# Splitting the weights of the feed-forward products between the two sides of SBUF

## The chip, the cores and the metric

The kernel runs on one core of a Trainium2 chip. The metric is the device time of one execution in microseconds (us). Engines: PE does the matmuls, DVE the elementwise work on vectors, ACT casts and activation functions, POOL a share of the elementwise work, and SP issues all the loads and stores (its queue is called SPq in the trace). Each engine works through its own instructions in a fixed order that was laid down when the program was built, and waits on semaphores of the others.

## The reference

One layer of an encoder for a sequence of 2048 tokens with 1024 channels, in float32: a windowed attention (16 query heads, 4 key heads, 128 tokens to either side, with a bias and a sink), and a dense feed-forward layer. Each of the two is wrapped in two RMS norms, with shift, scale and gate from a conditioning vector. The feed-forward, which the change touches, is

```
h = rmsnorm(x) * (1 + scale) + shift          # 2048 x 1024
a, b = split(h @ w_in)                        # first products, w_in 1024 x 5632
y = (silu(a) * b) @ w_out                     # last products, w_out 2816 x 1024
out = x + gate * rmsnorm(y)
```

## The kernel before, in words

All data lie transposed, channels on the 128 partitions. Every f32 operand of a product is split into a high and a low part (`split`, lines 153 to 155: ACT casts the high part, DVE subtracts it from the source for the low part), and one product of 128x128 weights with 512 tokens is then three matmuls (`three`, lines 147 to 151: high by high, high by low, low by high).

The products of the feed-forward are done by Strassen's scheme with seven products instead of eight. The class `Block` (line 731) is one output tile of both halves of the columns: it loads raw weights (`raw`, lines 737 to 740), forms the sums s1, s2, s3, s4 of their quarters on DVE (lines 744 to 747), splits seven weight tiles (line 752), and then does seven steps (`step`, line 755): step i multiplies weight a11, s2, a12, s3, s1, a22, s4 with operand b11, t2, b21, t3, t1, t4, b22, in this order, into one PSUM tile `pc0` to `pc6` out of a pool of six (`psC`). `take` evicts it.

* First products: class `Hidden` (line 779), 22 blocks for each half of the tokens, with four pairs of weight and operand tiles a step, so 12 matmuls a step and 84 a block. Names end in `i<half>_<block>`: `pc4_i0_1` is step 4 of block 1 of half 0, `wiri` is its raw weight tile, `ws1_i0_1` the split weight s1. Operands of half 0 are `hb110_k`, `ht20_k`, ..., four tiles each, loaded and split by `Operands.load` (line 724). In the trace they read `hb` and `ht`, since buffer numbers are left out.
* Last products: class `Outs` (line 921), for every part of the inner dimension (2 or 3 pairs of tiles, `MD` = 3 at most) four blocks; names end in `o<half>_<part>_<block>`. Results of the parts are added up in tiles `z<half>_<block>_<step>` (line 942).
* A tail `pl` (line 1077 on): the last part's products without Strassen's scheme for the last two column chunks, with weights `wl` and operands `gls`.

Ahead of the first products, PE ends the last output projection of the attention: eight tiles `py3_0` to `py3_7` (operands `ol3_k`, weights `wo`). Its pools stand on the right of SBUF and are closed at `lasto.close()` (line 882), so a tile that is opened on the right after it waits until these tiles are no longer read. Interleaved with the first blocks there is a background chain of DVE, POOL, ACT and a few matmuls (`late`, tiles `nhil`, `nstl`, `lr`, `ly`), the norms of the later column chunks; a tile `u2` and others of `take` stand in between on DVE.

SBUF is used as two stacks, left and right. In the first products the weights have two pools, `wi0` (left, open early) and `wi1` (right), which blocks use in turn, seven split tiles in each. Operands b11 and t2 lie in `hA` (left), b21 in its own pool and t3 with t1 in another (both left), t4 and b22 in `hB` (right). In the last products one ring of eleven split weight tiles is on the left, with operands b11 and t2; the other five operands are on the right. Left pools of the first products are closed after step 4 (of steps 0 to 6) of the last `Hidden` block, right ones after step 6; the loads for the last products into that place wait for it.

The order of all instructions on each engine is set by a scheduler that ranks by program order and by the offsets of `tc.high_priority`.

Of the kernel before, what the change touches and what calls it, by code (L numbers as in the profile page):

```python
# [18 lines left out]
P = 128  # L19
# [54 lines left out]
def encoder_layer(ctx, tc, a):  # L74
# [626 lines left out]
    wi = [open_pool(early, "wi0"), None]  # L701
    hA = open_pool(early, "hA", KT // 2)
    wbufs = 7
# [6 lines left out]
    class Operands:  # L710
# [20 lines left out]
    class Block:  # L731
# [3 lines left out]
        def __init__(self, ops, i, u, wa, wb):  # L735
            self.ops, self.u, m = ops, u, ops.m
            pl = wi[i % len(wi)]
# [10 lines left out]
            src = dict(sm_, a11=a11, a12=a12, a22=a22)  # L748
# [127 lines left out]
    b21p = open_pool(early, "b21", K2)  # L876
    t3p = open_pool(early, "t3", K2)
# [23 lines left out]
    for i in range(5):  # L901
        hid.step(i)
# [109 lines left out]
    with tc.high_priority(offset=400):  # L1012
        ops.load(*OPERANDS[2:])
# [22 lines left out]
    gs, wl = {}, []  # L1036
    for j in range(CPH):
        c = NCH - CPH + j
        for k in range(m):
            gs[c, k] = t = (hA if k < 2 else hB).tile([P, 2, CH], F32R, tag=OPERANDS[k], name=f"gls{c}_{k}")  # L1040
            sp.dma_start(f(t[:, 1]), g_d[-1][(t0 + k) // 2][f"b{k % 2 + 1}{j + 1}"])
            split(t[:, 0], t[:, 1], f(t[:, 1]), dve)
    for n in range(KT):
        raw = wi[0].tile([P, 2, 2 * MD * P], F32, tag="raw", name=f"wlr{n}").rearrange("p a b -> p (a b)")[:, :m * P]
        sp.dma_start(raw, a["w_out"][n, :, t0:t0 + m].rearrange("p k c -> p (k c)"))
        t = hB.tile([P, 2, CH], F32R, tag=("t1", "t4", "b22")[n // 3], name=f"wl{n}")
# [86 lines left out]
```

## Time and profile before

| what | value |
|---|---|
| median of three runs (2163.89, 2169.1, 2169.4) | 2169.1 us |
| the profiled execution | 2166.07 us, of it 2164.3 us span |
| PE busy | 2055.8 us (95% of the span) |
| DVE busy | 1649.8 us (76%) |
| ACT busy | 1076.4 us (50%) |
| POOL busy | 737.5 us (34%) |

Times within the profile count from the start of the span. The attention with its projections takes until about 821 us, the first products until 1688 us, the last products until 2098 us, the tail's matmuls until 2145 us, and then the last sums and stores. A row of the timeline has the start, the duration, the engine, the line, the operation, what it writes and reads, and how many alike it groups; in square brackets how long the engine sat idle before it and for whom. A row of the table by windows has the busy time and the count of instructions of each engine in a stretch, the granted clock of PE as a share of full speed, and what the DMA did.

### The profile page before, as it was taken

How to read it: one execution, taken by the hardware profiler on the slowest of the kernel's cores; microseconds unless marked ns; L12 is line 12 of the kernel's file. 1: busy time of each engine (PE TensorE's matmuls, PEld its weight loads, DVE VectorE, ACT ScalarE, POOL GpSimd, SP SyncE). 2: the span in 40 equal slices, each digit the busy share in tenths (PEclk: the TensorE clock that was granted, in tenths of full speed). 3: DMA queues.
4: the chain of work that ended last, by engine and by line, in shares of the span. 5: the costliest groups of instructions: out<-in, count | busy, mean ns of one | idle time of the engine just before them, and what ended most of it. 6: DMA issues, size and time to landing. Idle time of an engine off the chain costs nothing. (4 is left out here: it accounts for less than half of the span.)

```text
span 2164.3 us, 28995 instructions
## 1 busy us (share of the span) xinstructions
PE 2055.8 (95%) x9366; PEld 1666.6 (77%) x9366; DVE 1649.8 (76%) x2933; ACT 1076.4 (50%) x2125; POOL 737.5 (34%) x687
## 2 busy tenths in 40 slices
PE   6898999989989989999999999999999999998996
PEld 4786877878867768878887877888888788877886
DVE  7656767665676669876878897767673888999987
ACT  4546666577777746343434342333332844465422
POOL 3404343367778723434344422222221000220030
PEclk8999999999999989999999999999999999999998
DMA  8877665576667695545455764332231644438442
GB/s 279 261 254 253 184 182 175 159 282 233 227 199 245 189 347 206 183 148 162 138 178 194 257 220 142 112 106 94 98 117 54 210 153 138 141 129 280 161 132 103
DMA packets 200516, 396.35 MB, mean 183 GB/s; under 512 B 20091, under 2 KB 62124, under 8 KB 195244
## 3 DMA queue, kind: packets, MB, share of 16 engines
q1 hardware_dynamic: 199788, 393.97, 54.7%
q8 instruction: 74, 1.21, 0.2%
q14 instruction: 78, 0.64, 0.1%
q10 hardware_dynamic: 576, 0.52, 0.1%
HBM read 270.65 MB, written 123.76 MB: 182 GB/s over the span
## 5 line engine op out<-in xcount | busy, mean ns | idle before, releaser
L437 DVE CUSTOM_DVE_ANT_0 pr<-s,bias,nsink 128x384 f32<-128x384 f32 (+1 forms) x256 | 149.3, 596 | 91.5 <-PE s L432 74.3
L149 PE MATMUL pc_i<-ht,ws_i 128*128 128x512 f32 x528 | 207.2, 393 | 2.1 <-DVE b_i L799 1.5
L150 PE MATMUL pc_i<-ht,ws_i 128*128 128x512 f32 x528 | 206.9, 392 | 0.0
L151 PE MATMUL pc_i<-ht,ws_i 128*128 128x512 f32 x528 | 206.9, 392 | 0.0
L439 ACT ACTIVATE pr<-pr,nm 128x385 f32<-128x385 f32 (+1 forms) x256 | 153.8, 603 | 71.3 <-DVE nm L437 64.3
L815 POOL TENSOR_TENSOR p_i<-p_i,u_i 128x512 f32<-128x512 f32 x44 | 71.5, 1625 | 310.7 <-DVE u_i L802 153.6
L445 POOL TENSOR_SCALAR pr<-pr,rs 128x384 f32<-128x384 f32 (+1 forms) x256 | 147.4, 601 | 83.0 <-DVE rs L443 82.9
L946 POOL TENSOR_TENSOR z<-z,z 128x512 f32<-128x512 f32 x32 | 52.5, 1654 | 359.2 <-DVE z L942 342.3
L432 PE MATMUL s<-k,q 128*128 128x384 f32 (+1 forms) x512 | 136.1, 359 | 20.2 <-DVE nm L437 13.6
L149 PE MATMUL pc_i<-hb,wa_i 128*128 128x512 f32 x352 | 139.1, 395 | 2.0 <-DVE u_i L789 2.0
L150 PE MATMUL pc_i<-hb,wa_i 128*128 128x512 f32 x352 | 138.7, 394 | 0.0
L151 PE MATMUL pc_i<-hb,wa_i 128*128 128x512 f32 x352 | 138.7, 394 | 0.0
L155 DVE TENSOR_TENSOR plo<-t,phi 128x512 fp32r<-128x512 f32 x184 | 121.7, 685 | 16.2 <-ACT phi L154 14.7
L154 ACT CAST wa_i<-wiri 128x512 fp32r<-128x512 f32 x132 | 81.8, 620 | 102.2 <-PE pc_i L151 94.7
L154 ACT CAST ws_i<-s_i 128x512 fp32r<-128x512 f32 x132 | 81.6, 618 | 102.5 <-PE pc_i L151 98.7
L432 PEld LDWEIGHTS s<-k,q 128*128 128x128 f32 x512 | 86.6, 193 | 44.9 <-DVE nm L437 27.8
L149 PEld LDWEIGHTS pc_i<-ht,ws_i 128*128 128x128 f32 x528 | 99.3, 188 | 25.5 <-DVE b_i L799 2.2
L151 PEld LDWEIGHTS pc_i<-ht,ws_i 128*128 128x128 f32 x528 | 99.2, 188 | 22.4
L150 PEld LDWEIGHTS pc_i<-ht,ws_i 128*128 128x128 f32 x528 | 99.2, 188 | 22.2
L455 PE MATMUL t<-ident,pr 128*128 128x128 f32 x736 | 113.1, 273 | 3.1 <-POOL pr L445 2.4
L149 PE MATMUL py<-ol,wo 128*128 128x512 f32 x256 | 103.3, 405 | 11.9 <-ACT wo L154 7.4
L155 DVE TENSOR_TENSOR ws_i<-s_i,ws_i 128x512 fp32r<-128x512 f32 x132 | 104.6, 792 | 10.9 <-ACT ws_i L154 10.7
(320 smaller groups left out, 6142.8 us busy)
## 6 DMA issues: line engine op xcount, KB each, us to landing
wiri<-w_in SPq DMA_DIRECT2D x88, 512.0 KB, 4.8
ada<-ada_w SPq DMA_DIRECT2D x40, 512.0 KB, 4.9
wiro<-w_out SPq DMA_DIRECT2D x48, 384.0 KB, 3.9
q_d<-e SPq DMA_DIRECT2D x64, 256.0 KB, 3.9
q<-q_d SPq DMA_DIRECT2D x16, 1024.0 KB, 5.8
wo<-wo_d SPq DMA_DIRECT2D x16, 1024.0 KB, 5.7
g_d_b<-p_i SPq DMA_DIRECT2D x44, 256.0 KB, 4.7
g_d_t<-p_i SPq DMA_DIRECT2D x40, 256.0 KB, 2.0
```

The costliest lines, as they stand in the source:

```text
L149: pe.matmul(ps, w[0], h[0], start=first, stop=False)
L150: pe.matmul(ps, w[0], h[1], start=False, stop=False)
L151: pe.matmul(ps, w[1], h[0], start=False, stop=last)
L154: act.copy(hi, src)
L155: return eng.tensor_tensor(lo, src, f(hi), ALU.subtract).ins
L432: m = pe.matmul(ps[:, :n], q[:, h, jb * P:(jb + 1) * P], kk[:, i, (jb + j0) * P:(jb + j1) * P], start=i == 0, stop=i == 1)
L437: red = dve.tensor_tensor_reduce(pr[:, h, :n], ps[:, :n], bias[g][:, h, j0 * P:j1 * P], -1.0, nsink[:, hh:hh + 1], ALU.add, ALU.min, nm[:, ...
L439: act.activation(pr[:, h, :n + 1], pr[:, h, :n + 1], AF.Exp, bias=nm[:, h:h + 1], scale=-1.0, accum_out=rs[:, h:h + 1])
L445: pool.tensor_scalar(pr[:, h, :n], pr[:, h, :n], rs[:, h:h + 1], 1.0, ALU.mult, ALU.mult)
L455: pe.transpose(pt[:, h * P:(h + 1) * P], pr[:, h, jj * P:(jj + 1) * P], ident)
L815: pool.tensor_tensor(sa, sa, b, ALU.mult)
L946: (pool if (i, x) in ((2, 2), (4, 4), (5, 5), (6, 6)) else dve).tensor_tensor(sums[hf, n2, x], sums[hf, n2, x], sums[hf, n2, y], ALU.add)
```

## The change

In the first products each block's split weights now lie on both sides: those of steps 0 to 3 in `wl` (left, ring of 8) and those of steps 4 to 6 in `wr` (right, ring of 6). Only the raw weights and sums still alternate by block between a left pool `rw0` and a right pool `rw1`. Operands go with their weights: b11, t2, b21, t3 left, t1, t4, b22 right. The left pools are closed one step earlier, after step 3 (of steps 0 to 6) of the last block instead of step 4. In the last products the weights of steps 0 to 2 are on the left (`wl2`, ring of 5), those of steps 3 to 6 on the right (`wr2`, ring of 6), with b11, t2, b21 left and the other four operands right; the first block's right weights are split by a later call (`block.rest()`). In the tail the weights are held per pair of output tiles in two tiles, one for each side, and the operands of the last chunk are loaded after the weights. The numbers of matmuls, splits and bytes stay what they were. The core of the diff:

```diff
-    wi = [open_pool(early, "wi0"), None]
+    wl, wr = open_pool(early, "wl"), None
+    rw = [open_pool(early, "rw0"), None]
     hA = open_pool(early, "hA", KT // 2)
-    wbufs = 7
+    lbufs, rbufs, nleft = 8, 6, 4
...
         def slot(self, n, k):
-            pl = hA if n in ("b11", "t2") else b21p if n == "b21" else t3p if n in ("t3", "t1") else hB
-            t = pl.tile([P, 2, CH], F32R, tag=n, name=f"h{n}{self.u}_{k}")
+            t = (hA if n in OPERANDS[:nleft] else hB).tile([P, 2, CH], F32R, tag=n, name=f"h{n}{self.u}_{k}")
...
-            pl = wi[i % len(wi)]
+            pl = rw[i % len(rw)]
...
-            self.w = {}
-            for n, _ in self.STEPS:
-                w = pl.tile([P, 2, m, P], F32R, tag="w", bufs=wbufs, name=f"w{n}_{u}")
-                split(w[:, 0], w[:, 1], src[n], dve)
-                self.w[n] = w
+            self.src, self.w = dict(sm_, a11=a11, a12=a12, a22=a22), {}
+            self.split(wl, lbufs, self.STEPS[:nleft])
+            if wr is not None:
+                self.rest()
+
+        def rest(self):
+            self.split(wr, rbufs, self.STEPS[nleft:])
+
+        def split(self, pl, bufs, steps):
+            for n, _ in steps:
+                w = self.w[n] = pl.tile([P, 2, self.ops.m, P], F32R, tag="w", bufs=bufs, name=f"w{n}_{self.u}")
+                split(w[:, 0], w[:, 1], self.src[n], dve)
...
     lasto.close()
-    wi[1] = open_pool(ffn, "wi1", side="right")
+    wr = open_pool(ffn, "wr", side="right")
     hB = open_pool(ffn, "hB", K2, side="right")
+    rw[1] = open_pool(ffn, "rw1", side="right")
...
-    for i in range(5):
+    for i in range(nleft):
         hid.step(i)
     early.close()
...
-    wi = [open_pool(ctx, "wo", 2)]
+    wl, wr = open_pool(ctx, "wl2"), None
+    rw = [open_pool(ctx, "rw", 2)]
...
-    wbufs = 11
+    left, (lbufs, rbufs, nleft) = nleft, (5, 6, 3)
...
-        ops.load(*OPERANDS[:2])
+        ops.load(*OPERANDS[:nleft])
...
-    for i in range(5, 7):
+    for i in range(left, 7):
         hid.step(i)
     ffn.close()
-    hB = b21p = t3p = open_pool(ctx, "hB2", MD, side="right")
+    wr = open_pool(ctx, "wr2", side="right")
+    hB = open_pool(ctx, "hB2", MD, side="right")
...
     with tc.high_priority(offset=400):
-        ops.load(*OPERANDS[2:])
+        block.rest()
+        ops.load(*OPERANDS[nleft:])
```

What this makes of the order shows at three places. The first is the start of the first products. On SP (rows with the semaphores that they wait for; `ht10_k` is operand t1 of half 0, `ht40_k` t4, `hb220_k` b22, `y_d1` and `acc_d1` are stores of the attention's results), before, the operand t1 is loaded ahead of b11, t2 and t4, and its first two loads wait for matmuls of the output projection of the column chunk before the last:

```order
L728 DMA ht30_3_8768<-hd_d0_3_t3_317 128x512 [waits DMAHW1_49]
L728 DMA ht10_0_8772<-hd_d0_0_t1_306 128x512 [waits DMAHW2_49,PE_49]
L728 DMA ht10_1_8776<-hd_d0_1_t1_310 128x512 [waits DMAHW3_49,PE_49]
L728 DMA ht10_2_8780<-hd_d0_2_t1_314 128x512 [waits DMAHW4_49]
L728 DMA ht10_3_8784<-hd_d0_3_t1_318 128x512 [waits DMAHW5_49]
L728 DMA hb110_0_8699<-h2_d0_336 128x512 [waits DMAHW6_49]
```

and what waits for the last chunk's projection, whose tiles are on the right, is the load of t4, ten rows later; its third load waits for the last matmul that reads `ol3_3`:

```order
L728 DMA ht40_0_8788<-hd_d0_0_t4_307 128x512 [waits DMAHW0_49,PE_49]
L728 DMA ht40_1_8792<-hd_d0_1_t4_311 128x512 [waits DMAHW1_49,PE_49]
L728 DMA ht40_2_8796<-hd_d0_2_t4_315 128x512 [waits DMAHW2_49,PE_49]
L728 DMA ht40_3_8800<-hd_d0_3_t4_319 128x512 [waits DMAHW3_49]
L728 DMA hb220_0_8804<-h2_d1_337 128x512 [waits DMAHW4_49]
```

Now:

```order
L579 DMA y_d1_341<-y3_6_8641 128x512 [waits DMAHW1_49,Activation_49]
L730 DMA ht10_0_8772<-hd_d0_0_t1_306 128x512 [waits DMAHW2_49,PE_49]
L730 DMA ht10_1_8776<-hd_d0_1_t1_310 128x512 [waits DMAHW3_49]
L730 DMA ht10_2_8780<-hd_d0_2_t1_314 128x512 [waits DMAHW4_49]
L730 DMA ht10_3_8784<-hd_d0_3_t1_318 128x512 [waits DMAHW5_49]
L730 DMA ht40_0_8788<-hd_d0_0_t4_307 128x512 [waits DMAHW6_49]
L730 DMA ht40_1_8792<-hd_d0_1_t4_311 128x512 [waits DMAHW7_49,DVE_49]
L730 DMA ht40_2_8796<-hd_d0_2_t4_315 128x512 [waits DMAHW0_49]
L730 DMA ht40_3_8800<-hd_d0_3_t4_319 128x512 [waits DMAHW1_49]
L730 DMA hb220_0_8804<-h2_d1_337 128x512 [waits DMAHW2_49,DVE_49]
```

The loads of t1 stand behind those of b11 and t2, and the first of them waits for a matmul: for the last one that reads `ol3_3` in the output projection. Those of t4 and b22 follow it.

On DVE, at the same place, before (`ws1_i0_0`, `wa22_i0_0`, `ws4_i0_0`, the weights of steps 4 to 6 of block 0, stand 24 rows further up; here the low parts of t4 and b22):

```order
L155 TENSOR_TENSOR ht40_3_8800<-ht40_3_8800 128x512 [waits DMAHW3_49,Activation_49]
L155 TENSOR_TENSOR ws2_i0_2_9159<-s2_i0_2_9150,ws2_i0_2_9159 128x512 [waits Activation_49]
L155 TENSOR_TENSOR hb220_0_8804<-hb220_0_8804 128x512 [waits DMAHW4_49,Activation_49]
L155 TENSOR_TENSOR hb220_1_8808<-hb220_1_8808 128x512 [waits DMAHW5_49,Activation_49]
L789 TENSOR_TENSOR u2_i0_0_8882<-pc1_i0_0_8869,p1_i0_0_8867 128x512 [waits PE_49]
L155 TENSOR_TENSOR hb220_2_8812<-hb220_2_8812 128x512 [waits DMAHW6_49,Activation_49]
L155 TENSOR_TENSOR hb220_3_8816<-hb220_3_8816 128x512 [waits DMAHW7_49,Activation_49]
```

Now:

```order
L155 TENSOR_TENSOR ht40_0_8788<-ht40_0_8788 128x512 [waits DMAHW6_49,Activation_49]
L155 TENSOR_TENSOR ht40_1_8792<-ht40_1_8792 128x512 [waits DMAHW7_49,Activation_49]
L155 TENSOR_TENSOR ht40_2_8796<-ht40_2_8796 128x512 [waits DMAHW0_49,Activation_49]
L799 TENSOR_TENSOR p1_i0_0_8867<-pc2_i0_0_8884,p1_i0_0_8867 128x512 [waits DVE_49,PE_49]
L155 TENSOR_TENSOR ht40_3_8800<-ht40_3_8800 128x512 [waits DMAHW1_49,Activation_49]
L155 TENSOR_TENSOR hb220_0_8804<-hb220_0_8804 128x512 [waits DMAHW2_49,Activation_49]
L155 TENSOR_TENSOR hb220_1_8808<-hb220_1_8808 128x512 [waits DMAHW3_49,Activation_49]
L803 TENSOR_TENSOR u3_i0_0_8912<-pc3_i0_0_8899,u2_i0_0_8882 128x512 [waits PE_49]
L155 TENSOR_TENSOR hb220_2_8812<-hb220_2_8812 128x512 [waits DMAHW4_49,Activation_49]
L155 TENSOR_TENSOR hb220_3_8816<-hb220_3_8816 128x512 [waits DMAHW5_49,Activation_49]
L155 TENSOR_TENSOR ws1_i0_0_8845<-s1_i0_0_8826,ws1_i0_0_8845 128x512 [waits Activation_49]
L155 TENSOR_TENSOR wa22_i0_0_8848<-wiri0_0_8823,wa22_i0_0_8848 128x512 [waits Activation_49]
```

The three weight splits of block 0 stand behind all twelve operand splits of t1, t4 and b22 (the first four, with `u2_i0_0` among them, are the rows ahead of these), and behind three evictions. The eviction `u2_i0_1`, of step 1 of block 1, is row 1264 before and row 1275 now, and stands 28 rows behind the last but one split of b22 before, 44 rows behind `ws1_i0_0` now.

The second place is the switch to the last products, on SP: raw weights `wiro`, operands `hb11o`, `ht2o`, ... of the first part. Before:

```order
L739 DMA wiro0_0_1_15811<-w_out 128x512 [waits DMAHW6_49]
L740 DMA wiro0_0_1_15811<-w_out 128x512 [waits DMAHW7_49]
L728 DMA hb11o0_1_0_15985<-g_d0_2_b11_144 128x512 [waits DMAHW0_49]
L728 DMA ht2o0_1_0_16015<-g_d0_2_t2_145 128x512 [waits DMAHW1_49]
L739 DMA wiro0_0_2_15905<-w_out 128x512 [waits DMAHW2_49,DVE_49]
L740 DMA wiro0_0_2_15905<-w_out 128x512 [waits DMAHW3_49]
L728 DMA hb21o0_0_0_15708<-g_d0_0_b21_130 128x512 [waits DMAHW4_49,PE_49]
L728 DMA hb21o0_0_1_15712<-g_d0_1_b21_138 128x512 [waits DMAHW5_49,PE_49]
L728 DMA ht3o0_0_0_15716<-g_d0_0_t3_131 128x512 [waits DMAHW6_49]
```

Now:

```order
L730 DMA hb21o0_0_0_15618<-g_d0_0_b21_130 128x512 [waits DMAHW6_49]
L730 DMA hb21o0_0_1_15622<-g_d0_1_b21_138 128x512 [waits DMAHW7_49]
L741 DMA wiro0_0_1_15817<-w_out 128x512 [waits DMAHW0_49]
L742 DMA wiro0_0_1_15817<-w_out 128x512 [waits DMAHW1_49]
L730 DMA hb11o0_1_0_15991<-g_d0_2_b11_144 128x512 [waits DMAHW2_49]
L730 DMA ht2o0_1_0_16021<-g_d0_2_t2_145 128x512 [waits DMAHW3_49]
L730 DMA hb21o0_1_0_16051<-g_d0_2_b21_146 128x512 [waits DMAHW4_49]
L730 DMA ht3o0_0_0_15722<-g_d0_0_t3_131 128x512 [waits DMAHW5_49,PE_49]
L730 DMA ht3o0_0_1_15726<-g_d0_1_t3_139 128x512 [waits DMAHW6_49,PE_49]
L730 DMA ht1o0_0_0_15730<-g_d0_0_t1_132 128x512 [waits DMAHW7_49,PE_49]
```

The load of b21 now stands ahead of the raw weights of block 1 and waits for no PE instruction, that of t3 does. The first raw weights, `wiro0_0_0`, waited for a split of block 20 on DVE and wait now for step 3 of the last `Hidden` block on PE, with all left loads behind them.

The third place is on DVE in the last products, about the eviction `z1_0_0` of step 0 of a block, for which the matmuls of its step 1 (`pc1_o1_1_0`) wait. Before:

```order
L155 TENSOR_TENSOR ht1o1_1_2_18367<-ht1o1_1_2_18367 128x512 [waits DMAHW4_49,Activation_49]
L155 TENSOR_TENSOR ht4o1_1_0_18395<-ht4o1_1_0_18395 128x512 [waits DMAHW6_49,Activation_49]
L155 TENSOR_TENSOR ht4o1_1_1_18399<-ht4o1_1_1_18399 128x512 [waits DMAHW7_49,Activation_49]
L990 SCALAR_TENSOR_TENSOR zx1_0_18053<-z0_0_6_15809,coef_361,zx1_0_18053 128x512 [waits DMAHW0_49,DVE_49]
L942 TENSOR_TENSOR z1_0_0_17816<-pc0_o1_1_0_18474,z1_0_0_17816 128x512 [waits PE_49]
L990 SCALAR_TENSOR_TENSOR zx1_1_18058<-z0_0_4_15791,coef_361,zx1_1_18058 128x512 [waits DMAHW1_49,DVE_49]
L155 TENSOR_TENSOR ht4o1_1_2_18403<-ht4o1_1_2_18403 128x512 [waits DMAHW3_49,Activation_49]
```

Now:

```order
L155 TENSOR_TENSOR ht1o1_1_2_18373<-ht1o1_1_2_18373 128x512 [waits DMAHW5_49,Activation_49]
L155 TENSOR_TENSOR ht4o1_1_0_18401<-ht4o1_1_0_18401 128x512 [waits DMAHW7_49,Activation_49]
L950 TENSOR_TENSOR z1_0_0_17822<-pc0_o1_1_0_18480,z1_0_0_17822 128x512 [waits PE_49]
L155 TENSOR_TENSOR ht4o1_1_1_18405<-ht4o1_1_1_18405 128x512 [waits DMAHW0_49,Activation_49]
L999 SCALAR_TENSOR_TENSOR zx1_0_18059<-z0_0_6_15815,coef_361,zx1_0_18059 128x512 [waits DMAHW1_49,DVE_49]
L999 SCALAR_TENSOR_TENSOR zx1_1_18064<-z0_0_4_15797,coef_361,zx1_1_18064 128x512 [waits DMAHW2_49,DVE_49]
L155 TENSOR_TENSOR ht4o1_1_2_18409<-ht4o1_1_2_18409 128x512 [waits DMAHW3_49,Activation_49]
```

A final addition `zx1_0` and the split `ht4o1_1_1` stood ahead of it and stand behind it now.

More of the change, by code (lines that the diff above doesn't have):

```diff
@@ L875, in encoder_layer @@
     late = chain(late_residuals(), late_ada())
-    b21p = open_pool(early, "b21", K2)
-    t3p = open_pool(early, "t3", K2)
     half = Operands("0", K2, lambda n, k: hd_d[0][k][n] if n[0] == "t" else
@@ L1052, in encoder_layer @@
             if i < 2:
[L1053 removed]
+                pl, bufs = (wl, lbufs) if (i * KT + n) % (lbufs + rbufs) < lbufs else (wr, rbufs)
+                late_x[c, n] = load_x1(c, n, lambda name: f(pl.tile([P, 2, MD, P], F32R, tag="w", bufs=bufs, name=name)
                                                             .rearrange("p a k c -> p (a k c)"))[:, :CH])
@@ L1056, in encoder_layer @@
             for k in range(m):
-                w, g = wl[n], gs[c, k]
-                kc = slice(k * P, (k + 1) * P)
+                w, g = wo[n, k // 2], gs[c, k]
+                kc = slice(k % 2 * P, (k % 2 + 1) * P)
                 three(ps, (w[:, 0, kc], w[:, 1, kc]), (g[:, 0, cols], g[:, 1, cols]), k == 0, k == m - 1)
```

33 lines of the change are left out of this document (20 added, 13 removed).

## The prediction

> **What bounds the kernel now.** I read the page's busy times first, then PE's waits in the feed-forward (from 820 us on), then a table by windows around each wait.
>
> ```profile
> span 2164.3 us, 28995 instructions
> PE 2055.8 (95%) x9366; PEld 1666.6 (77%) x9366; DVE 1649.8 (76%) x2933; ACT 1076.4 (50%) x2125; POOL 737.5 (34%) x687
> ```
>
> PE's waits from 820 to 2145 us (total, times, longest):
>
> ```profile
> PE pc_o L149 <- DVE z L942: 6.5, 1, 6.5
> PE nstl L131 <- DVE nhil L129: 5.5, 2, 4.0
> ...
> PE pc_o L149 <- ACT hb21o L154: 1.7, 1, 1.7
> ```
>
> The windows (busy time and count of PE, PEld, DVE, ACT, POOL; the granted clock; DMA share and GB/s):
>
> ```profile
> 822.00:830.00 8.00, 8.00 (x37) 6.63 (x36) 7.06 (x10) 7.07 (x14) 2.72 (x2) 1.00 0.96 310
> 830.00:840.00 10.00, 10.00 (x46) 8.14 (x45) 10.00 (x18) 5.79 (x10) 0.96 (x1) 1.00 0.25 100
> 930.00:940.00 10.00, 8.79 (x39) 6.87 (x37) 8.83 (x11) 2.77 (x6) 5.71 (x4) 1.00 0.42 157
> 940.00:950.00 10.00, 7.17 (x21) 5.72 (x22) 7.56 (x12) 6.16 (x10) 3.04 (x2) 0.66 0.37 115
> 1688.00:1696.00 8.00, 5.50 (x22) 3.84 (x21) 7.93 (x16) 7.16 (x14) 3.13 (x2) 0.96 0.77 268
> 1696.00:1704.00 8.00, 8.00 (x31) 6.40 (x30) 6.85 (x14) 7.67 (x17) 0.00 (x0) 0.83 0.93 341
> 1920.00:1930.00 10.00, 7.71 (x26) 4.63 (x24) 10.00 (x12) 5.46 (x12) 5.67 (x4) 0.87 0.00 0
> 1970.00:1975.00 5.00, 4.71 (x21) 3.50 (x19) 5.00 (x10) 2.78 (x5) 0.00 (x0) 1.00 1.05 397
> 1975.00:1980.00 5.00, 0.00 (x0) 0.00 (x0) 5.00 (x10) 0.98 (x3) 0.00 (x0) 0.86 1.04 392
> 1980.00:1985.00 5.00, 3.78 (x9) 3.00 (x10) 5.00 (x9) 4.23 (x9) 0.00 (x0) 0.50 0.51 177
> 2000.00:2098.00 98.00, 98.00 (x425) 79.37 (x424) 90.84 (x150) 37.13 (x70) 20.50 (x14) 1.00 0.46 145
> ```
>
> PE is the bound: it is busy in 95% of the span, and 46 matmuls in 10 us (the window at 830) mean one each 0.2275 us, read off more finely from starts such as 820.79 and 821.03 below. What the change can win or lose after 821 us are PE's gaps, and each costs its wait and then some slow clock. Counting the matmuls that are missing against full pace: around 940 us 60 of 88 in 20 us, 28 x 0.2275 = 6.4 us for 4.0 us of waiting; around 1691 us 53 of 70 in 16 us, 3.9 us; at 1920, 18 missing, 4.1 us; from 1970 to 1985, 30 of 66, 8.2 us for 6.5 us of waiting. At the start of the first products, 822 to 840 us, PE waits for nothing: the windows' 8.00 and 10.00 are full. And DVE's busy time cannot change, since every split is still made; only its order does.
>
> **Start of the first products: t1 comes late.** The rows that carry this term: the timeline of SP, of DVE, and of PE at the change from the output projection (`py`) to block 0 (`pc_i`), and the loads and casts of `ht` from 800 to 850 us with their count, shortest, median and longest time in ns and their first and last start.
>
> ```profile
> 817.25 4.77 SPq L728 DMA_DIRECT2D ht<-hd_d_t  x4
> 822.07 1.85 SPq L728 DMA_DIRECT2D hb<-h_d  x4
> ```
>
> ```profile
> 813.96 4.89 DVE L155 TENSOR_TENSOR ht<-ht 128x512 fp32r<-128x512 f32 x8
> ...
> 831.29 1.28 DVE L155 TENSOR_TENSOR hb<-hb 128x512 fp32r<-128x512 f32 x2
> ...
> 850.55 0.67 DVE L789 TENSOR_TENSOR u_i<-pc_i,p_i 128x512 f32<-128x512 f32 x1
> ```
>
> ```profile
> 820.79 0.40 PE L151 MATMUL py<-ol,wo 128*128 128x512 f32 x1
> 821.03 0.39 PE L149 MATMUL pc_i<-hb,wa_i 128*128 128x512 f32 x1
> ```
>
> ```profile
> L728 SPq DMA_DIRECT2D ht<-hd_d_t x16: 319/376/454, 806.0 to 821.6; - x16
> L154 ACT CAST ht<-ht x16: 617/624/632, 812.3 to 827.4; 128x512 fp32r<-128x512 f32 x16
> ```
>
> Before, the low parts of t3 and t1 were the eight DVE instructions from 813.96 (8 in 4.89 us: 0.60 us from one to the next). Only t4 and b22 waited for the projection. Now t1 waits too, and as the queue is in order, all twelve loads of t1, t4 and b22 do. The last `py` matmul starts at 820.79; four matmuls of block 0 stand ahead of it now, so it ends near 822.1. The last `ht` load is issued at 821.6 and its cast starts at 827.4, 5.8 us later; so the first t1 cast starts at about 827.3 (it waits for no other cast) and its DVE split at 827.9. By the order, 15 DVE instructions stand from there to the split of `ws1_i0_0`: 15 x 0.60 = 9.0, so that starts at 836.9 and ends at 837.6. The loads don't limit this: they are issued each 0.46 us (1.85 for four). PE has 44 matmuls of steps 0 to 3 left when `py` ends and four that need no low part of a weight: 821.9 + 48 x 0.2275 = 832.8. It waits 4.8 us. ACT's casts of the same weights stand behind twelve casts of 0.52 us and a silu and so start no earlier than 833.5, which moves where in the step PE waits, not its end.
>
> The slow clock after it I take as 2.0 us, between 1.4 (3.9 less the 2.5 us of the two waits at 1691) and 2.4 (6.4 less 4.0 at 940).
>
> Then DVE is late. Between the third split of hb22 at 831.29 and `u2_i0_1` at 850.55 lie 28 instructions, 0.69 us each. Now 44 stand between `ws1_i0_0` and `u2_i0_1`: 836.9 + 44 x 0.69 = 867.3, ended at 867.9. PE's step 0 of block 2 waits for it (its PSUM slot), and reaches it after two blocks of 84: 821.03 + 168 x 0.2275 = 859.2, plus 4.8 + 2.0 = 866.0. Another 1.9 us. After block 3 the orders are alike again, and DVE has caught up, since it has idle time there. The term: 4.8 + 2.0 + 1.9 = +8.7 us; from +4 (the loads land 2 us sooner, DVE no longer late in block 2) to +13 (2.4 us of slow clock twice).
>
> [...]
>
> **Switch to the last products.** Before, hb21 was loaded once step 6 of the last `Hidden` block no longer held its place; PE waited for it.
>
> ```profile
> 1672.12 0.38 SPq L739 DMA_DIRECT2D wiro<-w_out  x1
> ...
> 1686.37 2.37 SPq L728 DMA_DIRECT2D hb21o<-g_d_b  x2
> ```
>
> ```profile
> 1675.43 0.43 DVE L155 TENSOR_TENSOR wa_o<-wiro,wa_o 128x256 fp32r<-128x256 f32 x1
> ...
> 1681.17 0.42 DVE L155 TENSOR_TENSOR wa_o<-wiro,wa_o 128x256 fp32r<-128x256 f32 x1
> 1681.50 0.42 DVE L155 TENSOR_TENSOR ws_o<-wiro,ws_o 128x256 fp32r<-128x256 f32 x1
> ...
> 1698.85 1.29 DVE L155 TENSOR_TENSOR hb22o<-hb22o 128x512 fp32r<-128x512 f32 x2
> ```
>
> ```profile
> 1688.22 0.39 PE L149 MATMUL pc_o<-hb11o,wa_o 128*128 128x512 f32 x1
> ```
>
> Now hb21 comes early, but the first raw weights, issued at 1672.12, wait for step 3 of that block, whose end I put at 1688.2, where PE begins the last products, less the 36 matmuls of steps 4 to 6: 1680.0; with all left loads they go out from 1680.4, 8.3 us later. Their first DVE work (1675.43, 3.3 us after the issue) moves to about 1683.9. From there DVE has for this block four sums and seven weight splits of 0.33 us (1681.17 to 1681.50; 3.7 in all), fourteen operand splits of 0.60 (8.4), five evictions of the last `Hidden` block (3.0) and, in between, the same 3.7 for the next block's weights: 18.8 us, to 1702.7, where hb22 before ended at 1700.1. PE's gap moves from step 2 to step 3. Half of the 2.6 us can hide, since block 1's work may stand behind; I take +1.5, from -3.9 (the gap closes, all of what the 1688 and 1696 windows miss) to +4.
>
> **Last products.** The rings are shorter (weight s4 of a block may be split once step 4 of the block before is done, not step 1), but DVE is the late one here, 5.00 of 5.00 busy in the windows from 1970 on, and the order hardly moves. At the long wait two instructions less stand ahead of the eviction that PE waits for:
>
> ```profile
> 1979.82 0.75 DVE L990 SCALAR_TENSOR_TENSOR zx<-z,coef,zx 128x512 f32<-128x512 f32 x1
> 1980.48 0.69 DVE L942 TENSOR_TENSOR z<-pc_o,z 128x512 f32<-128x512 f32 x1
> ```
>
> A split (0.60) and the addition `zx` (0.66, from 1979.82 to 1980.48): -1.3 us; from -12.3 (4.1 + 8.2, both waits gone) to +3. After 2000 us PE is busy 98.00 of 98.00; the tail's weights and operands are ready ahead of it in both orders, and its matmuls, evictions and stores are the same: 0, up to +2.
>
> **Sum:** 8.7 + 1.5 - 1.3 = +8.9 us on the profiled execution's 2166.07 (its span and 1.8 us around it): 2175.0. The median of the runs, 2169.1, is 3.0 above that execution, and the sum on it is 2178.0. I say 2176.5.
>
> **Rivals.**
> 1. *The start costs nothing in the end* (same). PE's later arrival is taken back at the gap at 940, worth 6.4 us, if the background chain to `nhil` keeps its time; the switch then gives 0. For it: that wait is on a chain of DVE, POOL and loads, not on the blocks. Against: DVE is what makes PE late, and the chain's `lr` stands later on DVE as well. 8.7 - 6.4 - 1.3 = +1.0: 2167 to 2170.
> 2. *A smaller DVE backlog in the last products* (faster). The gaps at 1920 and 1975 are one backlog of DVE. If DVE enters it with 6.5 us less behind PE, about 11 splits of 0.60, both close, -12.3 us; with the start at its low end, +4, and the switch at 0: -8.3, so 2158 to 2161. For it: b21 is split before PE needs it. Against: order and instructions between are nearly the same, and only two instructions moved.
> 3. *The lateness does not heal* (slower still). The chain of norms falls behind and the gap at 940 grows by 4 us, with the start at +11: about +14, 2180 to 2183.
>
> **Chances.** A change under 0.3% (6.5 us) can hardly be told from none here. My forecast is above that bound by 2.4 us; I give it, from 2171 to 2183, 0.50, of which 0.12 for its lower end lies within the bound. Rival 1 has 0.22 (0.02 of it with the wait at the switch closed too, and then faster), rival 2 0.15, rival 3 0.13. So faster 0.15 + 0.02 = 0.17, same 0.12 + 0.20 = 0.32, slower 0.38 + 0.13 = 0.51. The range leaves out rival 2 and the far part of rival 3: 2163 to 2188. The forecast's own is 2171 to 2183.
>
> **What would show it.** In the profile of the changed kernel: PE idle in 830 to 840 for 4 to 5 us, ended by the low part or cast of `ws_i`, with a granted clock below 1 behind; the `ht` loads grouped after 822; a wait on `u_i` near 866; at the switch a wait for `ht3o` in place of `hb21o`; the wait for `z` near 1984 about 5 us long. The step that fails first would be the first: no wait at 832 means that the loads went out earlier than the last projection allows, and then the time is rival 1's. A time under 2163 would mean that DVE's backlog, not the start, decides.

## The result, and the profile after

The changed kernel takes 2169.8 us (median of 14 runs, 2160.0 to 2175.1) against 2166.6 us for the kernel before on the same chip (14 runs, 2163.7 to 2173.8). The ratio is 1.0011 with a 95% interval of 0.9997 to 1.0024: no difference that can be told, where 2176.5 us had been predicted. The profiled execution of the changed kernel (2170.6 us) is 4.6 us longer than the one of before, although PE's busy time fell by 11.4 us. (VectorE, ScalarE and GpSimd are the engines DVE, ACT and POOL of the profile.)

```profile
span 2168.8 us, 28917 instructions
PE 2044.4 (94%) x9366; PEld 1669.0 (77%) x9366; DVE 1646.5 (76%) x2933; ACT 1076.9 (50%) x2125; POOL 747.7 (34%) x687
```

PE's longest waits from 820 to 2145 us, in the same view as before (in total, times, longest):

```profile
PE pc_o L149 <- DVE z L950: 8.1, 3, 6.8
PE nstl L131 <- DVE nhil L129: 6.0, 2, 3.7
PE pc_i L149 <- ACT ws_i L154: 5.2, 1, 5.2
PE pc_o L149 <- ACT z L947: 3.4, 1, 3.4
PE pc_i L149 <- ACT p_i L794: 3.3, 2, 2.1
...
PE pc_o L149 <- ACT ht3o L154: 2.4, 1, 2.4
```

The third, fourth and last are new. The windows that answer to those of before:

```profile
830.00:840.00 10.00, 4.76 (x15) 3.50 (x14) 8.26 (x14) 7.47 (x12) 0.00 (x0) 0.73 0.75 267
940.00:950.00 10.00, 7.92 (x35) 6.21 (x34) 9.99 (x13) 3.98 (x8) 4.49 (x3) 1.00 0.27 104
1696.00:1704.00 8.00, 5.09 (x16) 3.12 (x15) 8.00 (x18) 7.86 (x14) 5.33 (x1) 0.85 1.03 386
1980.00:1985.00 5.00, 2.08 (x10) 1.38 (x8) 5.00 (x10) 2.81 (x5) 0.00 (x0) 1.00 1.04 390
2000.00:2098.00 98.00, 98.00 (x434) 81.11 (x433) 94.25 (x160) 37.97 (x72) 15.81 (x10) 1.00 0.50 161
```

The last row holds the surprise. PE is busy for all 98 us in both kernels, and does 434 matmuls where it did 425. It is not waiting less, it is faster. A window also counts matmuls that began before it, so the pace is better read from the starts of steps. The timeline of PE before, first matmul of steps 6, 0 and 1 and then of 5, 6, 0 and 1 of the blocks that follow one another (12 matmuls a step):

```profile
1511.35 0.40 PE L149 MATMUL pc_i<-hb,ws_i 128*128 128x512 f32 x1
1514.15 0.40 PE L149 MATMUL pc_i<-hb,wa_i 128*128 128x512 f32 x1
1516.94 0.40 PE L149 MATMUL pc_i<-ht,ws_i 128*128 128x512 f32 x1
...
1528.14 0.39 PE L149 MATMUL pc_i<-ht,wa_i 128*128 128x512 f32 x1
1530.88 0.39 PE L149 MATMUL pc_i<-hb,ws_i 128*128 128x512 f32 x1
1533.61 0.39 PE L149 MATMUL pc_i<-hb,wa_i 128*128 128x512 f32 x1
1536.33 0.39 PE L149 MATMUL pc_i<-ht,ws_i 128*128 128x512 f32 x1
```

and after, steps 5, 6, 0 and 1:

```profile
1516.12 0.39 PE L149 MATMUL pc_i<-ht,wa_i 128*128 128x512 f32 x1
1518.84 0.39 PE L149 MATMUL pc_i<-hb,ws_i 128*128 128x512 f32 x1
1521.56 0.39 PE L149 MATMUL pc_i<-hb,wa_i 128*128 128x512 f32 x1
1524.29 0.39 PE L149 MATMUL pc_i<-ht,ws_i 128*128 128x512 f32 x1
```

Before, a step takes 2.80 us (233 ns a matmul) where its weights lie on the other side than its operand: steps 5 and 6 of blocks with weights on the left, steps 0 to 4 of those on the right. It takes 2.72 us (226.7 ns) where both lie on the same side. After, steps take 2.72 us throughout. This stood in the trace of before.

How late each place is against the profile of before shows where the time went. Taken is the start of the same VectorE instruction in both (the last eviction into `u2` of a first-products block, counted over both halves from 0; the first `z` addition of the last products and the last but one), in us:

```
                    block 0   block 3  block 12  block 21  block 42   first z  last but one z
before, start at     841.83    904.91   1081.47   1271.43   1668.96   1733.94   2099.49
changed kernel         +8.2      +8.7      +7.1     +10.3      +5.3     +13.1      +4.3
```

Each column compares two single executions; at places where two kernels are alike they differ by up to 2 us. The very last `z` addition is 7.0 us late, but PE's last matmul of the last products only 4.7 (2102.43 against 2097.72). The start costs 8.7 us. Then the pace gains 0.53 us for two blocks (from +8.5 at block 30 to +5.3 at block 42), about 12 us over 44 blocks if PE never waited, but between blocks 12 and 21 the kernel falls behind. At the switch 7.8 us are lost, and over the last products 8.7 won: 1200 matmuls there (24 blocks with five formerly mixed steps of nine, four with five of six) times 6 to 7 ns are 7 to 8.

### The profile page after: what moved, and what is told of

The parts are those of the page before. It is cut to its first block, busy times and chain, and to the rows that moved or that the text cites. A ratio compares the mean times of both kernels' runs of the same rounds, so it can differ in the third digit from the quotient of the medians.

```text
span 2168.8 us, 28917 instructions
## 1 busy us (share of the span) xinstructions
PE 2044.4 (94%) x9366; PEld 1669.0 (77%) x9366; DVE 1646.5 (76%) x2933; ACT 1076.9 (50%) x2125; POOL 747.7 (34%) x687
## 4 chain that ended last, share of the span: by engine, by line
PE 66%; DVE 15%; DMA 7%; issue 4%; ACT 3%; POOL 3%; SPq 1%; DVEq 0%; ACTq 0%; POOLq 0%
PE pc_i L149 10%; PE pc_i L150 10%; PE pc_i L151 10%; PE pc_o L151 4%; PE pc_o L149 4%; PE pc_o L150 4%; PE t L455 3%; PE s L432 3%; PE psq L149 2%; PE psq L151 2%; PE psq L150 2%; PE py L149 2%; PE py L151 2%; PE py L150 2%; PE o L461 2%
## 5 line engine op out<-in xcount | busy, mean ns | idle before, releaser
L155 DVE TENSOR_TENSOR wa_i<-wiri,wa_i 128x512 fp32r<-128x512 f32 x132 | 107.6, 816 | 5.4 <-ACT wa_i L154 5.1
```

The lines of the kernel that those rows point to most:

```text
L155: return eng.tensor_tensor(lo, src, f(hi), ALU.subtract).ins
```

## The experiments

**One half of the change at a time.** `e1_first` has the first products of the changed kernel and last products and tail of the kernel before; `e2_last` the reverse.

```diff
 # e1_first: lbufs, rbufs, nleft = 8, 6, 4 as changed; then, in the last products (first lines)
-    wl, wr = open_pool(ctx, "wl2"), None
-    rw = [open_pool(ctx, "rw", 2)]
+    wl, wr = open_pool(ctx, "wo", 2), None
+    rw = [wl]
 # e2_last: one pool of seven weights a block in the first products, as before; then
-    wi = [open_pool(ctx, "wo", 2)]
+    wl = open_pool(ctx, "wl2")
+    rw = [open_pool(ctx, "rw", 2)]
```

> Only the first-products part of the change; last products and tail as before. Theory S (side): a matmul whose weights and moving operand lie on different sides of SBUF starts its successor 6.6 ns later than one with both on the same side (2.80 against 2.72 us for a step of twelve). Then all steps of the first products take 2.72 us, the lag behind the kernel before is about +8.3 us after block 1, falls by about 0.27 us a block where PE does not wait, and is about +5 at block 42; the last products keep 2.10 us for steps 2 to 6 and 2.04 for steps 0 and 1 (nine matmuls). With 3 to 7 us lost at the switch: +8 to +12 us in all. Theory Q (waits only, that of the prediction): no pace differs, the lag stays at +8 to +9 until the switch, and the total is +9 to +12, without any difference in the steps.

> Only the last-products part of the change, with the tail; first products as before. Theory S: steps of the first products go on alternating between 2.72 and 2.80 us, all steps of the last products take 2.04 us; some 1200 matmuls of the last products lose 6.6 ns each, 7.9 us, and with a switch between -1 and +4 us the total is -4 to -9 us. Theory Q: only the two DVE instructions at the wait for z and the switch, -2 to +3 us, and steps 2 to 6 stay at 2.10.

`e1_first` took 2171.4 us (12 runs), ratio 1.0019 (1.0008 to 1.0030); `e2_last` 2160.7 us (8 runs), 0.9971 (0.9959 to 0.9983). So the half that was to cost about nothing gains 6 us, and the first half costs some 4, less than the 8 to 12 expected. In `e1_first` the first products run at 226.7 ns throughout and the last ones at 233 where mixed; in `e2_last` it is the other way round. The 8 us at the start and their price belong to the first half. The switch is no sum of the halves: from block 42 to the first `z` `e1_first` loses 1.9 us and `e2_last` wins 1.3, where the changed kernel's profile loses 7.8.

**Is it the pairing?** `e3_cross` is the changed kernel with the weights of the last products on the wrong sides.

```diff
-            self.split(wl, lbufs, self.STEPS[:nleft])
+            self.split(wl, lbufs, self.STEPS[lset])      # last products: steps 4 to 6 on the left
...
-            self.split(wr, rbufs, self.STEPS[nleft:])
+            self.split(wr, rbufs, self.STEPS[rset])      # last products: steps 0 to 3 on the right
```

> The changed kernel with the weights of the last products on the other sides: those of steps 0 to 3 on the right, of steps 4 to 6 on the left, operands where the change puts them. So steps 0, 1, 2, 4, 5, 6 have weights and operands apart, step 3 has both on the right. Theory S: step 3 takes 2.04 us, the six others 2.10, against 2.04 for all seven in the changed kernel, whatever the total does at the switch (some 9 us of slower matmuls). Theory Q, or a theory by which only the place of the operand counts: no step changes.

One run took 2185.1 us. All steps of its last products but one take 232 to 233.3 ns a matmul in the median, as the pairing has it. Step 3, with both on the right, takes 229 to 230 and not the 226.7 expected. Its matmuls, taken one by one, tell why the mean is between: most often the first 5 to 10 still start 224 to 239 ns apart, as in the mixed step ahead of it, and the others 226 to 227. So the pace follows the pairing and not the number of the step, but a matched step behind a mixed one takes some matmuls to get to its own pace. What carries over is not shown.

**Side, or address?** `e4_low` moves the right operands to the inner end of the right side, so that three of the four tiles of t1 lie wholly below address 128 KiB of a partition; by the built program of the changed kernel all four lie above it.

```diff
-    hB = open_pool(ffn, "hB", K2, side="right")
     rw[1] = open_pool(ffn, "rw1", side="right")
+    tmp = open_pool(ffn, "tmp", 10, side="right")
+    hB = open_pool(ffn, "hB", K2, side="right")
...
-    tmp = open_pool(ffn, "tmp", 10, side="right")
```

> The changed kernel with the operands t1, t4, b22 of the first products lowest on the right instead of below the weights: tiles 0, 2 and 3 of t1 then lie wholly below address 128 KiB of a partition, tile 1 with its high part just below and its low part above it, t4 and b22 above; their weights stay on the right. If what counts is the halves of the partition's address range (boundary at 128 KiB), eleven of the twelve matmuls of step 4 have weights and operand apart and the step takes 2.79 us, steps 5 and 6 stay at 2.72. If it is the distance between the two addresses or the stack that a pool belongs to, all three steps stay alike. The loads of t1 and t4 no longer lie over tiles of the last output projection, so the wait at 832 us should shrink from 5.2 to under 2 us: total -2 to -5 us against the changed kernel under S, with 3 us of slower matmuls in it.

2168.4 us (12 runs), 1.0006 (0.9994 to 1.0019). All steps keep 226.7 ns, t1's too, so neither the side of that address nor the distance between the two tiles sets the pace. The wait for `ws_i` shrinks from 5.2 to 2.0 us, but block 0 is still 7.3 us late: in this execution the last projection itself ends 3 us later (its last matmul starts at 824.12, in the changed kernel's at 821.15). The 2 to 5 us expected from the shorter wait did not come.

What differs between left and right is then this: by the built programs, all weight and operand tiles on the left begin at an address within the partition that leaves 96 modulo 256 bytes, all on the right one that leaves 224. `f_pad128` is the kernel *before* with one unused tile of 128 bytes on the right ahead of the feed-forward's pools, so that both leave 96; the order of instructions is the same row for row. `f_pad64` and `f_pad32` have 64 and 32 bytes. `f_apart` is the changed kernel with 128 bytes between its right weights and right operands: same side, another offset.

```diff
+    open_pool(ctx, "pad", 1, side="right").tile([P, 32], F32, name="pad")   # f_pad128; 16, 8 for 64, 32 bytes
     wi[1] = open_pool(ffn, "wi1", side="right")
```
```diff
     wr = open_pool(ffn, "wr", side="right")
+    open_pool(ffn, "pad", 1, side="right").tile([P, 32], F32, name="pad")   # f_apart
     hB = open_pool(ffn, "hB", K2, side="right")
```

> The kernel before with one unused tile of 128 bytes a partition opened on the right of SBUF ahead of the feed-forward's pools, so everything on the right from the first products on lies 128 bytes lower; nothing else moves, and the order on every engine is the same row by row. Theory S (side: weights and operand must lie on the same side): nothing changes, within 0.2%. Theory M (offset: what counts is that the addresses of weights and operand agree modulo 256; left tiles are at 96, right tiles at 224, and after this shift at 96 too): all steps of the first products take 2.72 us and of the last 2.04, so 22 x 7 steps x 0.08 = 12.3 us and 1200 x 6.6 ns = 7.9 us go: about 2147 us, ratio 0.991.

> The changed kernel with the unused 128 bytes between the right weights of the first products and what lies below them, so that in the first products the right weights stay at 224 modulo 256 and their operands t1, t4, b22 move to 96, on the same side as before. The order is that of the changed kernel. Everything on the right in the last products moves together with the 128 bytes, to 96 or stays, weights with operands. Theory S: nothing changes. Theory M: steps 4 to 6 of the first products take 2.80 instead of 2.72 us, 44 x 3 x 0.08 = 10.6 us, about 2180 us against the changed kernel's 2170.

> As the kernel with 128 unused bytes, with 64: right tiles at 160 modulo 256, left ones at 96. Theory M in the form that only bit 7 counts: 160 has bit 7 set, 96 not, so the steps with both apart stay at 2.80 us. In the form that the offsets must agree modulo 128 or be equal: the same or slower, between 2.80 and some more. Theory S: no change.

> As the kernel with 128 unused bytes, with 32: right tiles at 192 modulo 256, and so at a multiple of 64, left ones at 96. Theory M by bit 7: the steps with both apart stay at 2.80 us. If it is the alignment of each tile to 64 bytes that counts, the pace of steps with weights and operands both on the right changes too.

`f_pad128`: 2158.3 us (6 runs), 0.9958 (0.9942 to 0.9974); its timeline of PE, steps 5, 6, 0, 1 and the next block's 5:

```profile
1508.28 0.39 PE L149 MATMUL pc_i<-ht,wa_i 128*128 128x512 f32 x1
1511.00 0.39 PE L149 MATMUL pc_i<-hb,ws_i 128*128 128x512 f32 x1
1513.72 0.39 PE L149 MATMUL pc_i<-hb,wa_i 128*128 128x512 f32 x1
1516.44 0.39 PE L149 MATMUL pc_i<-ht,ws_i 128*128 128x512 f32 x1
...
1527.32 0.39 PE L149 MATMUL pc_i<-ht,wa_i 128*128 128x512 f32 x1
```

2.72 us for every step, with weights and operand on opposite sides. `f_apart`: 2176.0 us (6 runs), 1.0046 (1.0030 to 1.0061), and its steps 5 and 6 are slow again, on one side:

```profile
1517.82 0.39 PE L149 MATMUL pc_i<-ht,wa_i 128*128 128x512 f32 x1
1520.62 0.39 PE L149 MATMUL pc_i<-hb,ws_i 128*128 128x512 f32 x1
1523.40 0.39 PE L149 MATMUL pc_i<-hb,wa_i 128*128 128x512 f32 x1
```

`f_pad64` took 2160.8 us and `f_pad32` 2169.6, one run each. The medians, as the distance between the first matmuls of successive steps over the matmuls in a step, by where the weights start less where the operand starts, modulo 256:

```
offset (weights - operand)     ns per matmul   seen in
0                              226.7 to 228    changed kernel, f_pad128, g_best
0, behind a mixed step         226.7 to 232    before, e3_cross, f_apart, f_pad64, f_pad32
128                            232 to 234      before, f_apart, e3_cross
64  (weights 160, operand 96)  232.5 to 233.3  f_pad64
192 (weights 96, operand 160)  228.9 to 231    f_pad64
96 and 160                     232.5 to 235.6  f_pad32
```

The offset decides, and the side does nothing. (By the built programs, all starts that agree modulo 256 agree modulo 512 too, and no run has a pair 256 bytes apart, so the period could also be 512.) `f_apart` is at the same time the test on the changed kernel itself: with no instruction moved, the slow pace in three of the seven steps of its first products costs 7 to 8 us by the two ratios (1.0046 and 1.0011).

**Why 128 bytes gain 9 us and not 19.** PE in `f_pad128` arrives earlier where VectorE is the bound. The window from 1250 to 1300 us before, then of `f_pad128`, then of the changed kernel:

```profile
1250.00:1300.00 50.00, 47.53 (x204) 37.59 (x203) 50.00 (x77) 21.93 (x41) 13.69 (x9) 1.00 0.58 197
```
```profile
1250.00:1300.00 50.00, 44.41 (x188) 34.30 (x187) 50.00 (x78) 22.01 (x41) 12.34 (x8) 1.00 0.60 208
```
```profile
1250.00:1300.00 50.00, 43.16 (x181) 32.97 (x180) 50.00 (x80) 26.72 (x49) 9.37 (x6) 1.00 0.66 228
```

VectorE is busy for all 50 us in each, and PE, which was already 2.5 us short of work before, is short of 5.6 and 6.8. This is read from windows; no run took work off VectorE there. `f_pad128` is 2.1 us ahead at block 15 and 2.5 behind at block 24; there a faster PE waits longer. At the last but one `z` addition it is 8.9 us ahead.

**The start.** `g_away` opens the right pools of the changed kernel in another order, so that block 0's right weights don't lie where the last projection keeps its sums. Their splits then stand ahead of the twelve of t1, t4 and b22.

```diff
-    wr = open_pool(ffn, "wr", side="right")
-    hB = open_pool(ffn, "hB", K2, side="right")
     rw[1] = open_pool(ffn, "rw1", side="right")
+    tmp = open_pool(ffn, "tmp", 10, side="right")
+    wr = open_pool(ffn, "wr", side="right")
+    hB = open_pool(ffn, "hB", K2, side="right")
...
-    tmp = open_pool(ffn, "tmp", 10, side="right")
```

> The changed kernel, with the right side's pools opened in another order (the blocks' raw weights and the temporaries outermost, then the split weights, then the operands), so that block 0's right-hand split weights no longer lie where the last output projection keeps its sums, and their splits come ahead of the twelve splits of t1, t4 and b22 on VectorE and ScalarE. All offsets modulo 256 bytes stay as in the changed kernel. Theory P (the 8 us at the start are this place: the weights wait for memory, and therefore stand behind the twelve splits): the wait of 5.24 us at 832 is gone, block 0 is 1 to 3 us later than before the change where it was 8.2, and the kernel is 5 to 7 us shorter than the changed one if nothing takes it back, 2 to 4 if the waits on VectorE around blocks 12 to 21 take some. Rival D (the loads of the three right-hand operands themselves are late, whatever stands ahead of them): a wait of 4 to 5 us for t1 in the same place, block 0 still 7 to 8 us late, the time that of the changed kernel within 1.5 us.

2167.9 us (12 runs), 1.0004 (0.9990 to 1.0018). PE's waits from 820 to 910 us:

```profile
PE pc_i L149 <- ACT p_i L794: 4.7, 1, 4.7
PE pc_i L149 <- DVE b_i L807: 1.1, 1, 1.1
PE pc_i L149 <- ACT ws_i L154: 1.0, 2, 0.6
```

The wait of 5.2 us for `ws_i` is gone and block 0 is 4.0 us late, but the last eviction of block 1 is 10.1 late, a wait of 4.7 us has come in block 3, and block 3 is 10.6 late. (That wait is for ScalarE's copy of step 0, which stood behind an instruction of the background chain that had waited 9.65 us for VectorE's `ly`.) Neither theory holds as it was put: the weights' place made the first wait, and not the lateness. Windows of the stretch ahead show what else moved; before, after, and `g_away`:

```profile
780.00:822.00 42.00, 42.00 (x186) 34.73 (x185) 31.82 (x43) 26.46 (x45) 14.27 (x6) 0.99 0.95 340
```
```profile
780.00:822.00 42.00, 42.00 (x186) 34.68 (x185) 27.80 (x34) 24.02 (x40) 9.15 (x6) 1.00 0.74 263
```
```profile
780.00:822.00 42.00, 42.00 (x178) 34.41 (x178) 27.56 (x35) 24.69 (x40) 7.51 (x6) 0.95 0.84 306
```

VectorE does 4.0 us less ahead of the first products. By the order of the programs twelve instructions leave this stretch in the changed kernel: the four splits of t1 and three of weights, whose tiles are now on the right and not free, one more weight split, and the four sums of block 2; three splits of t2 come in. What has left it is made in the first blocks, where VectorE has no time left. This reading fits the three windows, each of one execution; no run gave VectorE just that work back and left the rest.

**The switch.** In the changed kernel, the rows of POOL, then SP, ACT and PE:

```profile
1698.66 13.34 POOL L823 TENSOR_TENSOR u_i<-u_i,b_i 128x512 f32<-128x512 f32 x1 [3.69 <-ACT u_i L819]
```
```profile
1699.95 0.33 SPq L742 DMA_DIRECT2D wiro<-w_out  x1
1712.03 0.33 SPq L778 DMA_DIRECT2D g_d_b<-u_i  x1
1712.40 0.43 SPq L730 DMA_DIRECT2D ht1o<-g_d_t  x1
```
```profile
1715.32 0.62 ACT L154 CAST ht1o<-ht1o 128x512 fp32r<-128x512 f32 x1 [6.08 <-DMA ht1o<-g_d_t]
1716.70 0.62 ACT L154 CAST ht4o<-ht4o 128x512 fp32r<-128x512 f32 x1 [0.76 <-DMA ht4o<-g_d_t]
1717.22 0.58 ACT L947 COPY z<-pc_o 128x512 f32<-128x512 f32 x1
```
```profile
1717.85 0.50 PE L149 MATMUL pc_o<-ht1o,ws_o 128*128 128x512 f32 x1 [3.45 <-ACT z L947]
```

GpSimd's last multiply, 1.3 us in the median of this tile's 44, takes 13.3; SP's store of its result waits for it, the loads of the next part's t1, t4 and b22 wait behind the store, ScalarE's casts for these loads, and the copy of `z`, which frees PE's PSUM slot, behind a cast. `g_mult` puts the two multiplies of that block on VectorE; `g_both` adds the pools of `g_away`.

```diff
-                pool.tensor_tensor(sa, sa, b, ALU.mult)
+                (dve if self.hf and self.t == HT - 1 else pool).tensor_tensor(sa, sa, b, ALU.mult)
```

> The changed kernel, with the last hidden block's two multiplies (silu times gate) on VectorE instead of GpSimd. Theory G (at the switch GpSimd's last multiply took 13.34 us instead of 1.3 because VectorE ran without a gap from 1698 to 1712; the store of its result stands on SP ahead of the loads of the next part's t1, t4 and b22, and ScalarE's casts of these ahead of the copies of z): SP's store and the three loads go 11 to 13 us sooner, the wait of 3.45 us at 1718 is gone, the lateness added at the switch falls from 7.8 us to about 3 to 4, and the kernel is 3 to 5 us shorter than the changed one. Rival V (VectorE is the bound there; it now has two instructions of 0.68 us more): the wait moves to VectorE's splits and the time stays within 1 us of the changed kernel's.

> The two edits together (the right side's pools in the other order, and the last hidden block's multiplies on VectorE). If P and G hold and the parts add: 8 to 11 us shorter than the changed kernel, about 2159 to 2162. If the waits on VectorE around blocks 12 to 21 take back what the start gains, as they did with the whole pace gain of the 128-byte pad: 4 to 6 us shorter, about 2164 to 2166. If D and V: as the changed kernel.

PE's waits from 1680 to 1735 us in `g_mult`:

```profile
PE pc_o L149 <- ACT ht1o L154: 2.5, 1, 2.5
PE pc_o L149 <- ACT ht3o L154: 1.0, 1, 1.0
```

The wait for `z` is gone, and from block 42 to the first `z` it loses 3.8 us where the changed kernel lost 7.8. But the time does not follow: 2169.4 us (11 runs), 1.0007 (0.9994 to 1.0019), against 1.0011 for the changed kernel. `f_apart`, whose engines have the changed kernel's order and whose multiply is still on GpSimd, suggests why: PE's longest wait at the switch, GpSimd's last multiply, and VectorE's split beside it are

```profile
PE pc_o L149 <- ACT ht3o L154: 2.8, 1, 2.8
```
```profile
1701.80 1.31 POOL L823 TENSOR_TENSOR u_i<-u_i,b_i 128x512 f32<-128x512 f32 x1 [1.10 <-ACT u_i L819]
```
```profile
1701.90 1.48 DVE L155 TENSOR_TENSOR ws_o<-s_o,ws_o 128x256 fp32r<-128x256 f32 x1
```

The multiply takes 1.31 us there, and 3.4 us are lost at the switch, no more than in `g_mult`. So the chain above is what happened in one execution of the changed kernel, and the multiply need not be long. Nor is it the only way to lose 7.8 us: `e4_low`, with a multiply of 1.46 us, loses as much by a wait of 7.5 us for `ht3o`, whose loads stand behind the store of the multiply's result there. How often the long multiply comes, the runs do not show.

`g_both` took 2166.3 us (11 runs), 0.9995 (0.9985 to 1.0004): between no gain and the sum, with intervals that overlap those of the changed kernel.

**What is best.** `g_best` is `e2_last` with the 128 bytes of `f_pad128`: first products in the old arrangement, without the lateness at the start, and equal offsets everywhere.

> The first products as before the change, the last products as after it, and 128 unused bytes at the bottom of the right side, so that weights and operand have the same offset modulo 256 bytes in every step, without the late weights at the start. Theory M (offset modulo 256): every step at 226.7 ns a matmul in both stages. If the gains of the two single runs add from where they arose (the pad gained 3.2 us up to the last products; the last products' own change gained 7.1 us behind that): about 10 us under before, 2156 to 2158. If the earlier arrival at VectorE-bound stretches takes back the last products' gain too: 2159 to 2161.

2154.1 us (5 runs), 0.9942 (0.9930 to 0.9954) of the kernel before: 12.6 us less by the ratio, the best of all. Every step of both stages takes 226.7 ns. It gains 4.0 us up to the first `z` and 8.3 behind it, a little more than the 3.1 of `f_pad128` and the 7.1 of `e2_last` in these places. The whole gains of those two runs, 9.1 and 6.3 us, do not add, since both hold the pace of the last products.

## Why the prediction was wrong

**The step that failed is this one: "46 matmuls in 10 us (the window at 830) mean one each 0.2275 us".** I took one pace for all matmuls, before and after, put the change's effect on it at nothing without a reason, and let only waits change. (Nor does the figure follow: 10 us over 46 are 0.217, as a window also counts matmuls that began before it.) The trace held two paces, 226.7 and 233 ns, and the change makes nearly all of them the faster one. That is worth about 19 us of PE's time (12 in the first products, 7 to 8 in the last), of which VectorE's full windows seem to have taken part back. The pace alone, in `f_pad128`, was worth 9.1 us. Put back onto the changed kernel's +2.4 (by the ratio) it gives a loss of 11.5 us, an estimate that takes the two as independent, where 8.9 had been summed: without the pace there would have been a loss, and with it there is no difference.

**Start, +8.7: right in size and place, wrong in cause, with some luck.** The loads went out from 821.58, as put; PE waited 5.24 us (4.8 predicted) for the cast of `ws1`:

```profile
836.76 0.79 PE L149 MATMUL pc_i<-ht,ws_i 128*128 128x512 f32 x1 [5.24 <-ACT ws_i L154]
...
841.57 0.40 PE L149 MATMUL pc_i<-ht,ws_i 128*128 128x512 f32 x1
```

The eleven matmuls from the first of these rows up to the second took 4.8 us (at a granted clock of 0.51) for 2.5 at full pace, so the slow clock cost 2.3 (2.0 predicted). The wait predicted near 866 came at 866.5 with 2.1 us (1.9), for ScalarE's copy `p_i` and not `u2`. Measured lateness at block 3: 8.7. That this is the predicted figure is luck in part: a wait of 1.2 us at 906 was not in the sum, and the faster pace, 0.27 us a block, gave about as much back. And I explained the lateness by the place of one split in a queue; `g_away` took that away, and as much lateness came by block 1.

**"DVE's busy time cannot change, only its order does"** held for the sum (1649.8 and 1646.5 us) and misled: at the start some 4 us of it moved out of a stretch where VectorE had idle time (31.8 of 42 us busy) into one where it had none (10.00 of 10 us busy from 830 to 840).

**Switch, +1.5: mis-sized.** Late raw weights and the wait for `ht3o` came as put, but the first issue was at 1685 and not 1680. It cost 3.4 us in `f_apart`'s execution, within my bounds of -3.9 to +4, and 7.8 in the changed kernel's, outside them, where GpSimd's long multiply and SP's store in front of the loads came on top; I had seen neither. (A slip of the sum: 1675.43 and 8.3 are 1683.7, not 1683.9.)

**Last products, -1.3:** of the 8.7 us won, 7 to 8 are pace, so what is left agrees in size. The mechanism is not shown: the long wait for `z`, which was to shrink from 6.5 to about 5 us, took 6.8 (to 1988.8, before to 1981.2).

**The rivals.** Rival 1's time (2167 to 2170) is what came, by another mechanism: the gap at 940 took nothing back (6.0 us for `nhil` against 5.5). Rival 2: VectorE's backlog did not close. Rival 3: the lateness did fall after block 21, by pace. The wide range held the time; the forecast itself, a loss that could be told from none, did not come.

## What to carry to other kernels

Before a change of addresses is costed, read the pace of PE per kind of step, from the first start of one to the first start of the next, and set it against the addresses of weights and operand. Here 128 unused bytes, with no instruction moved, gave 9 of the 12.6 us of the best version found. And a gain for PE is only worth what VectorE has left in the stretch where it lands, as the 9 us out of some 19 suggest. A long wait in one profile should be looked for in a second kernel of the same order before it is called the cause: the multiply of 13.3 us was one execution's.

## What the hardware showed that I had not expected

A 128x128 by 512 f32r matmul took 226.7 ns where weights and moving operand start at the same offset modulo 256 bytes (here also modulo 512), 229 to 236 ns at the other offsets tried. It is not symmetric: in `f_pad64`, 64 bytes one way cost 2 to 4 ns, the other way 6. And a matched step behind a mixed one ran its first 5 to 10 matmuls at the slow pace in `e3_cross`. No run shows the mechanism.

GpSimd's multiply of 128x512 took 13.3 us in one execution, where 1.3 is its median. VectorE's last row beside it and the next one:

```profile
1710.44 0.41 DVE L155 TENSOR_TENSOR ws_o<-s_o,ws_o 128x256 fp32r<-128x256 f32 x1
1715.97 0.69 DVE L155 TENSOR_TENSOR ht1o<-ht1o 128x512 fp32r<-128x512 f32 x1 [5.13 <-ACT ht1o L154]
```

VectorE worked without a gap up to 1710.85; the multiply, begun at 1698.66, ended at 1712.00, 1.15 us into the gap, about its usual length. In the pair of rows of `f_apart` above it went the other way: the multiply took 1.31 us, and VectorE's split, begun 0.10 us after it, 1.48 instead of the 0.41 here. So in each of these two executions one of the two ran long. No run tests why, or what decides which of the two it is.
